# Low halves of weights made by accumulating transfers, a reload on another queue, and 32-row operands padded to 128 rows

## The chip, the core and the metric

The kernel runs on one core of a Trainium2 chip. The core has a matrix engine (TensorE, PE in the profile), a vector engine (VectorE, DVE), a scalar engine (ScalarE, ACT), a general engine (GpSimd, POOL) and SyncE (SP), which here only issues transfers. Each engine works through its own queue of instructions in order; semaphores order them among each other. Sixteen DMA engines carry the transfers; SP's go through hardware queues, POOL's through a queue that its software fills. The metric is the device time of one execution in microseconds, the median of the runs.

## The reference

One layer, in float32, for a prompt of 512 tokens and 32 sample tokens (8 sequences of 4), 544 columns in all:

```python
x = x + 0.5 * swiglu(rms_norm(x), ffn1_gate, ffn1_up, ffn1_down)
h = rms_norm(x)
z = h @ w_in            # q, k, v of 8 attention heads; q, f, i and gate of 4 recurrent heads
x = x + concat(moba(q_a, k_a, v_a), gate * norm(hgrn2(q_b, f_b, i_b))) @ w_out
x = x + 0.5 * swiglu(rms_norm(x), ffn2_gate, ffn2_up, ffn2_down)

def swiglu(x, w_gate, w_up, w_down):
    return (silu(x @ w_gate) * (x @ w_up)) @ w_down
```

The model width is 1024, the hidden width of the feed-forward nets 2816. `moba` is attention; the sample tokens attend to 1024 past keys and values that lie in a paged cache (pages of 128, found through a page table), and to the sequence's own new ones. `hgrn2` is a gated linear recurrence with a state of 128 x 128 per head. New keys, values and states are outputs too.

## The kernel before

Activations stand transposed: 128 features on the partitions, 544 columns, in two halves of 272. Every large product in float32 is made of three products in a faster format: a number is split into a high part (rounded to that format) and a low part (the rest), and high x high, low x high and high x low are summed in PSUM (`products`, line 608). So PE runs chains of 272-column matrix products `xh,whi`, `xl,whi`, `xh,wlo`.

A weight block of 128 x 512 numbers (256 KB) is a unit. SP loads it into a tile `raw` (`w_load`, line 516), ACT casts it into `whi`, and DVE subtracts, `wlo = raw - whi`:

```python
def split_unit(self, src, nk, x):                       # line 530
    hi, lo = self.take_slot(x, (F32R, F32R))
    nc.scalar.copy(hi[:, :nk], src[:, :nk])
    nc.vector.tensor_tensor(lo[:, :nk], src[:, :nk], hi[:, :nk].bitcast(F32), op=ALU.subtract)
```

`w_pump` (line 572) keeps up to four split units (`AHEAD`) ready before PE asks for them. In the feed-forward nets the gate and up products of the first five hidden blocks are plain (two units each); from block 5 on (`NREG`) gate and up are done together as seven products in place of eight ("paired": `paired_gemm`, line 645), which needs sums of four weight quarters, `S` (two on DVE, two on POOL, in `w_split`, line 537), and sums of activation tiles (`right_factors`, line 661, whose steps `PACE` spreads over time).

The mixing layer (400 to 787 us) multiplies by `w_in` (28 jobs of two units), runs the attention and the recurrence as their columns arrive, and multiplies by `w_out` (8 jobs of two units). For the sample tokens POOL gathers 32 tiles of K and 32 of V, 128 x 1024 each, from the paged cache (`KV<-cache_k,idx`, `KV<-cache_v,idx`). Small products there: `kn`,`qh` and `kn`,`ql` are the prompt's scores, per pair of heads; `KV,PT` the sample's weighted values from the cache, `vs,PO` those of its own new values (32 rows); `s,hqp` the recurrence's output from the state, `hVs,ats` from its own new values (32 rows); `fc,y_qk` spreads the root factors of 32 tokens over the columns. At the layer's end the residual that was spilled after FFN 1 is reloaded, `y<-xs` (line 1769), by POOL's queue.

The order of all instructions is set before the kernel is built, by a planner inside the kernel's own program (`Order`, `Engine`, `Pool`): it simulates the engines with modelled costs, and writes each engine's instructions out in the order of modelled start times. A transfer costs its engine 0.06 us in this model. The profile attributes all instructions to one line, 284, where they are issued; so they are told apart by their tiles.

## Time and profile before

| | us |
|---|---|
| median of 3 runs (lowest to highest) | 1205.38 (1205.19 to 1206.52) |
| the profiled execution | 1210.65 |
| its span on the core | 1208.9 |
| PE busy | 1178.1 (97%) |
| DVE busy | 858.5 (71%) |
| ACT busy | 551.9 (46%) |
| POOL busy | 228.3 (19%) |
| DMA: SP's queue / POOL's queue, share of the 16 engines | 30.6% / 9.1% |

The span is what lies between the first and the last instruction of the core; the execution's time is 1.75 us longer. A matrix product of 272 columns is listed with 0.29 us, but products overlap: the next starts 0.125 us later. Stages: reading of x and start 0 to 20 us, FFN 1 to 400, the mixing layer 400 to 787, FFN 2 from 787 on.

### The profile page before, as it was taken

The numbers are of one execution on the slowest core, as the hardware profiler recorded it, in microseconds if no ns is written. First come the engines' busy times: TensorE is split into PE (matmuls) and PEld (weight loads), VectorE is DVE, ScalarE is ACT, GpSimd is POOL, SyncE is SP. The second block draws the span as 40 slices with busy tenths as digits, with TensorE's granted clock in tenths as the row PEclk, the third lists the DMA queues.
The fourth block names the chain that finished last, engine by engine and source line by source line (L and its number), as shares of the span: only waits on it lengthen the run. The fifth ranks groups of instructions, "written<-read, shape, count | busy, mean of one in ns | idle before, by whom it ended". The sixth has DMA issues, their size and how long they took to land.

```text
span 1208.9 us, 26320 instructions
## 1 busy us (share of the span) xinstructions
PE 1178.1 (97%) x10571; PEld 1113.7 (92%) x10571; DVE 858.5 (71%) x1729; ACT 551.9 (46%) x1125; POOL 228.3 (19%) x211
## 2 busy tenths in 40 slices
PE   8999999999999999989999999899999999999998
PEld 8989999999999988878878867799999999999998
DVE  6988559954875698877776557667977488736843
ACT  6455246532654345554556433344554266524632
POOL 3012012200202401000332344220020023102200
PEclk9999999999999999989999999899999999999999
DMA  5244453333314642322565776352344323323222
GB/s 161 79 123 114 133 148 97 97 106 87 87 54 135 193 129 69 97 72 74 181 195 160 235 262 222 111 158 79 93 118 131 97 81 104 106 87 88 63 79 82
DMA packets 216238, 144.74 MB, mean 120 GB/s; under 512 B 12035, under 2 KB 204067, under 8 KB 216116
## 3 DMA queue, kind: packets, MB, share of 16 engines
q1 hardware_dynamic: 205588, 106.60, 30.6%
q0 software_dynamic: 10432, 36.32, 9.1%
q8 instruction: 83, 1.36, 0.5%
q14 instruction: 39, 0.32, 0.1%
q10 hardware_dynamic: 96, 0.14, 0.0%
HBM read 133.94 MB, written 11.83 MB: 121 GB/s over the span
## 4 chain that ended last, share of the span: by engine, by line
PE 77%; DVE 13%; ACT 3%; DMA 3%; issue 2%; SPq 1%; POOL 0%; DVEq 0%; ACTq 0%; POOLq 0%
PE mm L284 51%; PE sm L284 26%; DVE wlo L284 3%; DVE xl L284 2%; DVE xwl L284 1%; DMA raw<-ffn_down 1%; ACT xh L284 1%; DVE t_h L284 1%; SPq L284 1%; ACT whi L284 1%; DVE hl L284 1%; ACT sq L284 1%; DMA raw<-ffn_up 1%; DVE S L284 1%; DMA KV<-cache_v,idx 1%
## 5 line engine op out<-in xcount | busy, mean ns | idle before, releaser
L284 PE MATMUL mm<-xh,whi 128*128 128x272 f32 x1216 | 365.0, 300 | 1.0 <-DVE t_g L284 0.5
L284 PE MATMUL mm<-xl,whi 128*128 128x272 f32 x1216 | 352.4, 290 | 5.4 <-DVE xl L284 5.2
L284 PE MATMUL mm<-xh,wlo 128*128 128x272 f32 x1216 | 353.2, 290 | 1.1 <-DVE wlo L284 1.1
L284 ACT CAST whi<-raw 128x512 fp32r<-128x512 f32 (+1 forms) x230 | 138.7, 604 | 261.4 <-PE mm L284 192.3
L284 PEld LDWEIGHTS mm<-xh,whi 128*128 128x128 f32 x1216 | 231.5, 190 | 18.2 <-issue 15.7
L284 PEld LDWEIGHTS mm<-xl,whi 128*128 128x128 f32 x1216 | 231.3, 190 | 6.4 <-DVE xl L284 6.2
L284 PEld LDWEIGHTS mm<-xh,wlo 128*128 128x128 f32 x1216 | 231.0, 190 | 2.1 <-DVE wlo L284 2.1
L284 DVE TENSOR_TENSOR wlo<-raw,whi 128x512 fp32r<-128x512 f32 (+1 forms) x230 | 165.1, 727 | 81.0 <-ACT whi L284 77.4
L284 POOL TENSOR_TENSOR S<-raw,raw 128x512 f32<-128x512 f32 x18 | 30.4, 1691 | 380.9 <-DMA raw<-ffn_up 261.1
L284 PE MATMUL mm<-hh,whi 128*128 128x272 f32 x352 | 101.5, 288 | 0.3 <-DVE x L284 0.3
L284 PE MATMUL mm<-hh,wlo 128*128 128x272 f32 x352 | 101.1, 287 | 0.0
L284 PE MATMUL mm<-hl,whi 128*128 128x272 f32 x352 | 101.1, 287 | 0.0
L284 PE MATMUL mm<-xwh,xh 128*128 128x272 f32 x296 | 85.4, 288 | 1.3 <-DVE t_h L284 0.8
L284 PE MATMUL sm<-xwl,xh 128*128 128x272 f32 x296 | 85.3, 288 | 0.0
L284 PE MATMUL mm<-xwl,xh 128*128 128x272 f32 x296 | 85.3, 288 | 0.0
L284 PE MATMUL sm<-xwh,xh 128*128 128x272 f32 x296 | 85.2, 288 | 0.0
L284 PE MATMUL mm<-xwh,xl 128*128 128x272 f32 x296 | 85.2, 288 | 0.0
L284 PE MATMUL sm<-xwh,xl 128*128 128x272 f32 x296 | 85.2, 288 | 0.0
L284 DVE TENSOR_TENSOR xl<-S,xh 128x512 fp32r<-128x512 f32 x84 | 66.0, 796 | 4.1 <-ACT xh L284 3.7
L284 PEld LDWEIGHTS mm<-hh,whi 128*128 128x128 f32 x352 | 66.3, 188 | 0.7 <-ACT whi L284 0.5
L284 ACT CAST xh<-S 128x512 fp32r<-128x512 f32 x84 | 51.8, 620 | 32.7 <-DVE S L284 13.7
L284 PEld LDWEIGHTS mm<-hh,wlo 128*128 128x128 f32 x352 | 66.2, 188 | 0.0
(325 smaller groups left out, 2639.2 us busy)
## 6 DMA issues: line engine op xcount, KB each, us to landing
raw<-ffn_down SPq DMA_DIRECT2D x64, 256.0 KB
raw<-ffn_gate SPq DMA_DIRECT2D x56, 256.0 KB
raw<-ffn_up SPq DMA_DIRECT2D x56, 256.0 KB
raw<-w_in SPq DMA_DIRECT2D x56, 256.0 KB
raw<-ffn_down SPq DMA_DIRECT2D x32, 192.0 KB
xl<-ffn_gate SPq DMA_DIRECT2D x16, 256.0 KB
xh<-ffn_up SPq DMA_DIRECT2D x16, 256.0 KB
xl<-ffn_up SPq DMA_DIRECT2D x16, 256.0 KB
```

Of the source, the lines that this page charges most:

```text
L284: call(*map(real, args), **{k: real(v) for k, v in kw.items()})
```

## The change

1. *Low parts.* For the 72 units of `w_in` and `w_out`, and for the second unit of the plain gate and up jobs of both feed-forward nets (18 units), the low part is no longer subtracted by DVE. ACT writes `-raw`, rounded to the fast format, into `wlo`, and POOL issues a transfer that adds `raw` to it. In the mixing layer up to six units are made ahead (`AHEAD_MIX`).
2. *Paired jobs.* They now hold five `raw` tiles. Two of the four sums are DVE additions in place, one is a POOL sum, and one is an accumulating transfer; signs are turned accordingly in `hidden_paired`. `right_factors` makes its tiles in other pieces (a class `Factors`; 14 DVE operations, of which more are half as wide, in place of 10, and `PACE` 1.1 in place of 0.8).
3. *The reload* `y<-xs` goes to SP's queue.
4. *Padding.* `vs`, `hVs`, `ats` and `PO` get 128 partitions, of which the upper 96 are filled with zeros once; the products with them, and the one with `y_qk`, run with 128 rows.
5. Of the first hidden block, `up` is read from PSUM directly (two DVE copies less); the planner's model has other costs for transfers issued by POOL; the base of weight slots grows from 4 to 6, and the memory for POOL's descriptors is set to 8192 bytes.

```diff
 HT = T // 2
-PACE = 0.8
+AHEAD_MIX = 6
+PACE = 1.1
...
-                s = self.order.dma(self.part, 4 * args[1].shape[0] * self.free(args[1]), names)
+                pool = self.part == "pool"
+                s = self.order.dma(self.part, 4 * args[1].shape[0] * self.free(args[1]), names,
+                                   1.3 if pool else 0.06, 3.0 if "accum_op" in kw else 1.5)
...
-        self.nc.sync.dma_start(raw[:, :job["nk"]], job["src"][len(job["raw"])])
+        raw_k = raw[:, :job["nk"]]
+        i = len(job["raw"])
+        if job["paired"]:
+            parts = [r[:, :job["nk"]] for r, _ in job["raw"]]
+        if job["src"][i] is None:
+            self.nc.gpsimd.tensor_tensor(raw_k, parts[0], parts[1], op=ALU.add)
+        else:
+            self.nc.sync.dma_start(raw_k, job["src"][i])
+            if job["paired"] and i == 2:
+                self.nc.gpsimd.dma_start(raw_k, parts[0], accum_op=ALU.add)
+        if job["paired"] and i == 3:
+            self.nc.gpsimd.dma_start(parts[1], raw_k, accum_op=ALU.add)
...
-    def split_unit(self, src, nk, x):
+    def split_unit(self, src, nk, x, transfer=False):
+
         nc = self.nc
         hi, lo = self.take_slot(x, (F32R, F32R))
         nc.scalar.copy(hi[:, :nk], src[:, :nk])
+        if transfer:
+            nc.scalar.activation(lo[:, :nk], src[:, :nk], AF.Identity, scale=-1.0)
+            nc.gpsimd.dma_start(lo[:, :nk], src[:, :nk], accum_op=ALU.add)
+            return hi, lo, x
         nc.vector.tensor_tensor(lo[:, :nk], src[:, :nk], hi[:, :nk].bitcast(F32), op=ALU.subtract)
...
-            self.units.append(self.split_unit(job["raw"][n][0], nk, x))
+            self.units.append(self.split_unit(job["raw"][n][0], nk, xs[0], job["mixer"] or n == 1 and job["start"]))
...
-            nc.tensor.matmul(p3[64 * h:64 * h + 64, :NS], r[96:128, 18 + h:19 + h].to_broadcast([NS, 64]),
-                             self.ident[96:128, 96:128], start=True, stop=True)
+            nc.tensor.matmul(p3[:, NS * h:NS * h + NS], r[:, 18 + h:19 + h].to_broadcast([128, 128]),
+                             self.ident[:, 96:128], start=True, stop=True)
...
-        self.vs = mp.tile([NS, 512], F32, name="vs")
+
+        self.vs = mp.tile([128, 512], F32, name="vs")
+        self.Vs = mp.tile([128, 128], F32, name="hVs")
+        self.ats = mp.tile([128, 2 * NS], F32, name="ats")
+        self.PO = mp.tile([128, 128], F32, name="PO")
+        for x in (self.vs, self.Vs, self.ats, self.PO):
+            nc.gpsimd.memset(x, 0.0)
...
-                nc.gpsimd.dma_start(x[k], xspill[k])
+                nc.sync.dma_start(x[k], xspill[k])
...
-    nc = bacc.Bacc("TRN2", target_bir_lowering=False, num_devices=1)
+    nc = bacc.Bacc("TRN2", target_bir_lowering=False, num_devices=1, dynamic_dma_scratch_size=8192)
```

How this moves instructions is shown at three places. Numbers behind a tile's name only tell copies apart.

DVE at the third pair of attention heads, before (`z` are columns of the projection, `kn` the normed keys that PE waits for, `ql` low parts of the queries):

```order
L284 TENSOR_TENSOR z_6991<-mm_6822,R_5311 128x272
L284 TENSOR_TENSOR z_6991<-mm_6925,R_5311 128x272
L284 TENSOR_TENSOR wlo_7005<-raw_6742,whi_6954 128x512
L284 TENSOR_TENSOR wlo_7016<-raw_6751,whi_6977 128x512
L284 SCALAR_TENSOR_TENSOR kn_1288_7010<-sm_6997,qkg,kn_1288_7010 64x512
L284 TENSOR_TENSOR ql_7027<-qn_6937,qh_1289_6994 64x512
L284 SCALAR_TENSOR_TENSOR kn_1290_7025<-sm_6997,qkg,kn_1290_7025 64x512
```

The same place after:

```order
L288 TENSOR_TENSOR z_6996<-mm_6859,R_5322 128x272
L288 TENSOR_TENSOR ql_7008<-qn_6934,qh_1245_6990 64x512
L288 TENSOR_SCALAR KS<-sm_7019,qkg 128x32
L288 SCALAR_TENSOR_TENSOR kn_1244_7023<-sm_7013,qkg,kn_1244_7023 64x512
L288 SCALAR_TENSOR_TENSOR kn_1246_7030<-sm_7013,qkg,kn_1246_7030 64x512
L288 TENSOR_TENSOR ql_7008<-qn_6934,qh_1247_7005 64x512
```

The two subtractions that stood ahead of `kn` are gone from DVE's queue there, and `KS`, the sample's keys, has come ahead of it.

ACT at the second pair of heads, before (`kt` keys, `qh` high parts of the queries):

```order
L284 COPY kt_6490<-sm_6444 128x512
L284 COPY kt_6490<-sm_6463 128x128
L284 CAST whi_6521<-raw_6210 128x512
L284 CAST whi_6548<-raw_6361 128x512
L284 CAST qh_1195_6560<-qn_6440 64x512
L284 ACTIVATE kn_1194_6575<-sm_6562,qkg 64x512
```

The same place after:

```order
L288 CAST whi_6548<-raw_6420 128x512
L288 ACTIVATE wlo_6558<-raw_6420 128x512
L288 CAST whi_6576<-raw_6439 128x512
L288 ACTIVATE wlo_6584<-raw_6439 128x512
L288 ACTIVATE kn_1158_6591<-sm_6579,qkg 64x512
```

Behind each cast of a weight tile stands now the negation into `wlo`, so four instructions on weights stand ahead of `kn` in place of two.

POOL between the gathers of V for the sample tokens, before:

```order
L284 DMA KV_9798<-cache_v,idx 128x1024
L284 DMA KV_10037<-cache_v,idx 128x1024
L284 DMA KV_10058<-cache_v,idx 128x1024
L284 DMA KV_10085<-cache_v,idx 128x1024
L284 DMA KV_10122<-cache_v,idx 128x1024
L284 TENSOR_TENSOR at_10171<-oS_9967,fc 128x512
```

And in the changed kernel, at a like place:

```order
L288 DMA KV_9840<-cache_v,idx 128x1024
L288 DMA wlo_9777<-raw_9318 128x512
L288 DMA wlo_9864<-raw_9335 128x512
L288 DMA KV_9888<-cache_v,idx 128x1024
L288 DMA wlo_9928<-raw_9480 128x512
L288 DMA wlo_10006<-raw_9509 128x512
L288 DMA KV_10081<-cache_v,idx 128x1024
```

The accumulating transfers of low parts stand in POOL's queue between the gathers, here four around one gather.

## Rows read from the trace of the kernel before

Instructions of the kernel before; times in us from the span's start unless marked ns.

**Rows 1.** The page's part 1 (busy time, share of the span, instructions of each engine) and part 4 (the chain that ended last, by engine):

```profile
PE 1178.1 (97%) x10571; PEld 1113.7 (92%) x10571; DVE 858.5 (71%) x1729; ACT 551.9 (46%) x1125; POOL 228.3 (19%) x211
...
PE 77%; DVE 13%; ACT 3%; DMA 3%; issue 2%; SPq 1%; POOL 0%; DVEq 0%; ACTq 0%; POOLq 0%
```

**Rows 2.** The table by stretch: start and end, length, then busy us (and instructions) of each engine, TensorE's granted clock, share of the DMA engines, GB/s:

```profile
20.00:60.00 40.00, 39.67 (x315) 39.10 (x315) 34.08 (x72) 20.08 (x36) 6.01 (x5) 1.00 0.25 69
60.00:120.00 60.00, 57.12 (x440) 55.25 (x439) 52.74 (x88) 33.06 (x66) 10.84 (x8) 1.00 0.45 120
160.00:400.00 240.00, 239.68 (x1910) 239.03 (x1910) 174.48 (x284) 118.25 (x229) 46.40 (x32) 1.00 0.34 98
440.00:580.00 140.00, 134.68 (x1012) 117.64 (x1011) 115.02 (x297) 72.84 (x173) 11.18 (x11) 0.95 0.29 85
580.00:690.00 110.00, 109.00 (x1414) 89.44 (x1416) 76.16 (x196) 57.84 (x137) 37.59 (x42) 1.00 0.63 195
690.00:760.00 70.00, 67.09 (x1079) 50.71 (x1079) 44.56 (x122) 21.97 (x59) 30.25 (x32) 1.00 0.72 239
760.00:787.00 27.00, 21.51 (x218) 19.46 (x217) 16.51 (x42) 10.41 (x27) 4.80 (x9) 0.87 0.31 92
...
845.00:920.00 75.00, 73.06 (x579) 72.39 (x578) 63.50 (x109) 39.00 (x75) 10.73 (x8) 1.00 0.38 109
```

**Rows 3.** The same table for two stretches inside the mixing layer whose granted clock is 0.50:

```profile
531.60:541.80 10.20, 8.78 (x29) 7.03 (x30) 7.12 (x22) 3.82 (x11) 0.00 (x0) 0.50 0.28 79
767.10:773.90 6.80, 4.37 (x19) 4.37 (x20) 5.14 (x13) 0.65 (x1) 0.00 (x0) 0.50 0.12 35
```

**Rows 4.** The timeline of PE at two places with small products (start, us, line, operation, tiles, rows and columns of the array used, shape):

```profile
466.88 0.42 PE L284 MATMUL sm<-s,hqp 128*32 128x128 f32 x8
467.24 0.42 PE L284 MATMUL sm<-hVs,ats 32*32 32x128 f32 x8
...
468.30 0.71 PE L284 MATMUL sm<-hV,at 128*128 128x128 f32 x4
...
762.58 1.52 PE L284 MATMUL sm<-KV,PT 128*32 128x128 f32 x48
```

**Rows 5.** Groups of PE's instructions by line and shape (count, busy us and mean ns of one, idle time before them and its cause):

```profile
L284 PE MATMUL sm<-vs,PO 32*32 32x128 f32 x64 | 4.2, 279 | 0.8 <-issue 0.6
...
L284 PE MATMUL sm<-hVs,ats 32*32 32x128 f32 x64 | 3.4, 280 | 0.0
...
L284 PE MATMUL sm<-fc,y_qk 32*64 32x32 f32 x16 | 1.2, 228 | 0.0
```

**Rows 6.** Groups of instructions by line and shape on DVE, ACT and POOL, columns as in the group before:

```profile
L284 DVE TENSOR_TENSOR wlo<-raw,whi 128x512 fp32r<-128x512 f32 x198 | 147.3, 755 | 63.3 <-ACT whi L284 59.9
L284 ACT CAST whi<-raw 128x512 fp32r<-128x512 f32 x198 | 122.2, 619 | 228.8 <-PE mm L284 172.0 <-issue 34.7 <-DVE y_n L284 5.0
L284 POOL DMA_INDIRECT KV<-cache_v,idx x32 | 31.5, 984 | 43.5 <-PE sm L284 40.0 <-issue 1.2 <-PE mm L284 0.8
L284 POOL TENSOR_TENSOR S<-raw,raw 128x512 f32<-128x512 f32 x18 | 30.4, 1691 | 380.9 <-DMA raw<-ffn_up 261.1 <-PE mm L284 52.6 <-DVE wlo L284 41.3
```

**Rows 7.** The table by stretch for the subtractions that write `wlo` alone (DVE's busy time and their count, granted clock, DMA share, GB/s):

```profile
440.00:580.00 140.00, 19.06 (x24) 0.95 0.29 85
580.00:690.00 110.00, 10.69 (x14) 1.00 0.63 195
690.00:760.00 70.00, 4.87 (x7) 1.00 0.72 239
```

**Rows 8.** Timelines of DVE and then of PE at the third pair of heads (in brackets the idle time before, and what ended it):

```profile
527.95 2.65 DVE L284 TENSOR_TENSOR wlo<-raw,whi 128x512 fp32r<-128x512 f32 x2
530.62 0.74 DVE L284 SCALAR_TENSOR_TENSOR kn<-sm,qkg,kn 64x512 fp32r<-64x512 f32 x1
...
529.54 0.29 PE L284 MATMUL mm<-xh,wlo 128*128 128x272 f32 x1
533.02 0.55 PE L284 MATMUL sm<-kn,qh 128*128 128x256 f32 x1 [3.19 <-DVE kn L284]
```

**Rows 9.** Timelines of DVE and of PE at the end of the mixing layer:

```profile
765.09 0.69 DVE L284 TENSOR_TENSOR wlo<-raw,whi 128x512 fp32r<-128x512 f32 x1
...
769.53 0.59 PE L284 MATMUL mm<-xl,whi 128*128 128x272 f32 x1 [3.10 <-DVE xl L284]
```

**Rows 10.** The group of POOL's instructions that reload `y`:

```profile
L284 POOL DMA_DIRECT2D y<-xs x8 | 4.4, 580 | 22.2 <-PE mm L284 22.2
```

**Rows 11.** DMA queue 0 in 690 to 760 us (the one POOL issues to: packets, MB, share of 16 engines), the gathers issued there, and the chain of waits there by line:

```profile
q0 software_dynamic: 4015, 14.62, 61.2%
...
KV<-cache_v,idx POOLq DMA_INDIRECT x29
...
by line: PE sm L284 46.0%; PE mm L284 19.2%; DMA KV<-cache_v,idx 9.3%; issue 5.4%; DVE sst L284 3.6%; ACT SC L284 2.9%; DVE hkh L284 1.6%; POOL KV L284 1.3%; DVE hqh L284 1.1%; DVE hs L284 1.1%; DVE hf L284 1.1%; DVE sq L284 1.0%; DVE rec L
```

**Rows 12.** The timeline of POOL among the gathers of V:

```profile
707.54 0.94 POOL L284 DMA_INDIRECT KV<-cache_v,idx  x1 [0.72 <-PE sm L284]
709.12 0.94 POOL L284 DMA_INDIRECT KV<-cache_v,idx  x1 [0.65 <-PE sm L284]
```

**Rows 13.** The timeline of POOL (its last four sums of squares) and of PE (the first product of the next unit) at the start of FFN 1:

```profile
19.30 6.85 POOL L284 TENSOR_TENSOR sqsum<-sqsum,sq 128x544 f32<-128x544 f32 x4 [0.71 <-ACT sq L284]
...
27.51 0.29 PE L284 MATMUL mm<-xh,whi 128*128 128x272 f32 x1
```

More of the change, by code (lines that the diff above doesn't have):

```diff
@@ L455, in quarters, with turns, job @@
                     for r in (r0, r0 + h)]
-        def plain(m, nk, r0, c0):
-            out.append({"paired": False, "src": quarters(m, nk, r0, c0), "nk": nk // 2, "raw": [], "done": 0})
-        def ffn(p):
+        def turns(m, nk, r0, c0):
+            rows = m[128 * r0:128 * (r0 + nk), c0:c0 + 128].rearrange("(k two p) m -> two p k m", two=2, p=128)
+            return [rows[0], rows[1]]
+        def job(kind, src, nk):
+            out.append({"kind": kind, "src": src, "nk": nk // 2, "raw": [], "done": 0, "paired": kind is not None, "mixer": False})
@@ L461, in ffn, with plain, paired @@
+        def plain(m, nk, r0, c0, mixer=False, start=False):
+            job(None, quarters(m, nk, r0, c0), nk)
+            out[-1]["mixer"] = mixer
+            out[-1]["start"] = start
+        def paired(kind, nk, a11, a12, a21, a22, transfer):
+            job(kind, [a11, a21, a21 if transfer else None, a22, a12], nk)
+            out[-1]["transfer"] = transfer
+        def ffn(p, pairs):
             gate, up, down = (a[p + n][0] for n in ("_gate", "_up", "_down"))
-            for g0, ng in FGROUPS:
+            for g0, ng in FGROUPS[pairs]:
@@ L463, in ffn @@
                 for f in range(g0, g0 + ng):
                     if f < NREG:
-                        plain(gate, KD, 0, 128 * f)
-                        plain(up, KD, 0, 128 * f)
-                    else:
-                        out.append({"paired": True, "nk": KD // 2, "raw": [], "done": 0,
-                                    "src": quarters(gate, KD, 0, 128 * f) + quarters(up, KD, 0, 128 * f)})
-                for m in range(KD):
-                    plain(down, ng, g0, 128 * m)
-        ffn("ffn1")
+                        plain(gate, KD, 0, 128 * f, start=True)
@@ new lines, in ffn @@
+                        plain(up, KD, 0, 128 * f, start=True)
+                    else:
+                        paired("a", KD, *quarters(gate, KD, 0, 128 * f), *quarters(up, KD, 0, 128 * f), pairs)
+                for m in range(0, KD, 2):
+                    if pairs:
+                        paired("a", ng, *turns(down, ng, g0, 128 * m), *turns(down, ng, g0, 128 * (m + 1)), True)
+                    else:
+                        plain(down, ng, g0, 128 * m)
+                        plain(down, ng, g0, 128 * (m + 1))
@@ L474, in weight_jobs @@
+        ffn("ffn1", False)
         for n, j in IN_ORDER:
-            plain(a["w_in"][0], KD, 0, COLS[n] + 128 * j)
+            plain(a["w_in"][0], KD, 0, COLS[n] + 128 * j, True)
         for m in range(KD):
-            plain(a["w_out"][0], KD, 0, 128 * m)
-        ffn("ffn2")
+            plain(a["w_out"][0], KD, 0, 128 * m, True)
+        ffn("ffn2", False)
         return out
     def room(self, kind, job):
-        free = [x for x in self.slots[kind] if x["used"] < x["bufs"] and (x["extra"] is None or job["paired"])]
+        free = [x for x in self.slots[kind] if x["used"] < x["bufs"] and x["extra"] in (None, job["kind"])]
@@ L572, in w_pump, with ahead @@
     def w_pump(self):
-        while (len(self.units) < AHEAD and self.w_split()) or self.w_load():
+        def ahead():
+            mixer = self.splitting < len(self.jobs) and self.jobs[self.splitting]["mixer"]
+            return len(self.units) < (AHEAD_MIX if mixer else AHEAD)
+        while (ahead() and self.w_split()) or self.w_load():
             pass
@@ L654, in paired_gemm @@
             for k in range(nk):
-                xh, xl = xw[k]
-                self.products(ps[b], w, k, xh[:, r], xl[:, r], first and k == 0, k == nk - 1, not first)
+                f = xw[k]
+                self.products(ps[b], w, k, f.hi(r), f.lo(r), first and k == 0, k == nk - 1, not first)
                 yield
@@ L852, in ffn, with add @@
                 yield from self.gemm(xg, KD, up)
+            if pairs:
+                for m in range(0, KD, 2):
+                    yield from self.paired_gemm(hs, ng // 2, self.down_paired(pool, x, m, done if last else lambda m: None))
+                continue
             yield from self.settle()
-            if g0 + ng == NFF:
+            if last:
                 self.fewer_slots()
             for m in range(KD):
-                def add(p, h, m=m):
+                def add(p, h, m=m, last=last):
                     c = self.cols(h)
                     nc.vector.scalar_tensor_tensor(x[m][:, c], p, 0.5, x[m][:, c], op0=ALU.mult, op1=ALU.add)
-                    if h and g0 + ng == NFF:
+                    if h and last:
                         done(m)
                 yield from self.gemm(hs, ng, add, both=m == 0)
+        if pairs:
+            self.fewer_slots()
     def setup(self):
```

260 lines of the change are left out of this document (161 added, 99 removed).

## The prediction, made before the changed kernel ran

> **What bounds the kernel now.** I read the shares of the engines and of the chain first. [rows 1] TensorE (PE) is busy 1178.1 of 1208.9 us and 77% of the chain that ended last is PE; VectorE (DVE) follows with 13%. So an edit pays only where PE waits, or where PE's own instructions become cheaper. The table by stretch then shows where PE waits [rows 2]: in the steady part of the first feed-forward net (160 to 400 us) not at all, 239.68 of 240 us, and there, as in its like in the second, nothing that the change moves can show. PE is idle for 0.33 us in 20:60, 2.88 us in 60:120, 1.94 us in 845:920, and, in the mixing layer, 5.3 us in 440:580, 1.0 us in 580:690, 2.9 us in 690:760, 5.5 us in 760:787. That is some 20 us, plus what the clock costs: two stretches of 10.2 and 6.8 us show a granted clock of 0.50, the lower of its two levels, 1.2 against 2.4 GHz [rows 3]. Both begin inside the longest waits of PE in the layer [rows 8, 9]. The sum below is made against the profiled execution, 1210.65 us (span 1208.9 and 1.75 around it); the median of the three timed runs, 1205.38, is 5.3 lower, and I subtract the same change from it.
>
> **The change, part by part.**
>
> *Padded operands.* The products with `vs`,`PO` and `hVs`,`ats` (32 partitions) and the broadcast of `y_qk` get 128 rows. Their number stays. What changes is seen in the starts on PE [rows 4]: groups of eight `s,hqp` (128 rows) and eight `hVs,ats` (32 rows) alternate, four groups from 466.88 to 468.30, thus 0.355 us per group with one change of row count each. Forty-eight `KV,PT`, all of 128 rows, take 1.52 us, of which about 0.27 is the length of the last, so 1.25 / 47 = 0.027 us each, and eight would take 0.21. A change of row count therefore costs about 0.355 - 0.21 = 0.14 us. There are 64 records of `vs,PO` in groups of eight, 64 of `hVs,ats` in groups of eight, and 16 of `y_qk` in groups of four [rows 5]: 20 groups, 40 changes, 40 x 0.14 = 5.6 us at most. I take 0.11 each, -4.4 us, since a group with other operands may pay something of it anyway. Ends: -5.6 to 0 (a loss is excluded: the number of products stays, and 128 rows run at 0.027 us a start). The Trainium skill speaks against this term: "TensorE: Matmul & The Clock Gate", section "Why this matters for your kernels", has a single matmul of 32 rows take the same time as one of 128. By that rule alone the term is nothing and the sum 4.4 us smaller; the durations in the rows agree with it, the starts between groups do not, and I go by the starts.
>
> *Low parts in the mixing layer.* 72 units lose a DVE subtraction and gain an ACT negation and an accumulating transfer on POOL's queue. A subtraction takes 0.76 us and ACT's cast 0.62 [rows 6]; there are 24 in 440:580, 14 in 580:690, 7 in 690:760 [rows 7]. DVE is off PE's path for most of them, so 72 x 0.76 = 55 us of DVE do not come back as time. Three places do.
> First, the third pair of heads [rows 8]: DVE runs two subtractions from 527.95 that last 2.65 us, and only then `kn`, at 530.62; PE, done with its projection at 529.54, waits 3.19 us for `kn`. In the new order nothing of the weights stands ahead of this `kn`, on DVE or on ACT. 2.65 us are gone; what is late next is `kn`'s own ACT step and 0.74 us on DVE, about the time PE arrives. I take -2.7 (0 to -3.2).
> Second, the clock. The 10.2 us at 0.50 begin at 531.6, inside that wait [rows 3, 8], and hold 8.78 us of PE work, of which half, 4.4 us, is the low level. Whether the level still falls when PE pauses there for some tenths of a microsecond only, these rows don't tell. I take half, -2.2 (0 to -4.4).
> Third, the end of the layer [rows 9]: a subtraction of 0.69 us at 765.09 stands in DVE's row ahead of the last head's root and `xl`, for which PE waits 3.10 us until 769.53. Its place can go: -0.7 (0 to -0.7; ACT's `xh` may be late next, since ACT now has a negation there).
>
> *What this adds.* ACT gets 72 x 0.62 = 45 us in 387; at 52% in 440:580 it has room [rows 2], but ahead of the second pair's `kn` it now runs cast, negation, cast, negation. POOL gets 72 issues of 0.58 (the plain reload) to 0.98 us (a gather) [rows 6, 10], in one queue with the gathers: a low part waits behind a gather that waits for PE to free its tile, and a gather behind a low part that waits for ACT. The transfers themselves are not in the trace. In 690:760, 29 gathers and little else took 61.2% of 70 us of all engines by POOL's DMA queue [rows 11], 1.5 us each for 512 KB (128 x 1024 numbers), so a low part of 256 KB takes 0.75 us, or 1.5 if its second reading counts like a transfer. In 580:690, 14 of them ask 10 to 21 us, and 0.37 x 110 = 41 are free: hidden, and PE has work (0.99 busy). In 690:760, 7 ask 5 to 10 us where 0.28 x 70 = 20 are free, but the gathers of V run without a gap there, 1.6 us apart [rows 12], and 9.3% of the chain, 6.5 us, is their transfers. Here I take +2 (0 to +10).
>
> *The starts of the feed-forward nets.* 18 low parts leave DVE, 13 us of work that is nearly all beside PE: PE's idle time there is 0.33 + 2.88 + 1.94 us [rows 2]. Against it stand about 1.6 us more in `right_factors` (an estimate: 14 DVE operations in place of 10 on each of four tiles, most of them half as wide, 0.4 us a tile) and, in each paired job, one POOL sum of 1.69 us replaced by a transfer [rows 6]. I take -1 (-3 to +2). In FFN 1 the first low part is issued behind POOL's last sum of squares, which ends at 26.15 us [rows 13], and the plain product after it begins at 27.51: an issue and a transfer of 0.6 + 0.75 us and their way are late by +1 (0 to +2).
>
> *No cost.* The reload of `y` moves from POOL (4.4 us in all, after 22 us of waiting for the layer's pools) to SP [rows 10]; the products of `w_out`, whose inputs are ready, stand on PE while it runs. The zero fills run once on POOL while it is idle. If the reload is late, PE's first sum of FFN 2 shows it: 1 to 2 us, taken into the range.
>
> The sum: -4.4 - 2.7 - 2.2 - 0.7 + 2 - 1 + 1 = -8.0, so 1202.6 for a profiled execution and **1197.4** for the median.
>
> **The rivals.**
> *A, the V gathers become the bound (slower).* For it speaks that they already follow each other without a gap and that POOL's order now has low parts in pairs between them; against it, that 46 of 70 us of the chain there are PE's. Each of 7 low parts would push the gathers by its issue and its transfer, 0.98 + 1.5 = 2.5 us: +17 instead of +2. It decides once the transfers' share in 690:760, now 0.72, comes near 1. Sum: -8 + 15 = +7, 1212.4.
> *B, nothing comes of it.* The wait for `kn` only changes its owner, ACT's negations in place of DVE's subtractions, the clock falls as before, and the padding gives nothing: -8.0 + 2.7 + 2.2 + 4.4 = +1.3, 1206.7. ACT's new order at the second pair of heads speaks for it, the third pair's against it.
> *C, only the padding's term is nothing.* -8.0 + 4.4 = -3.6, 1201.8. The equal durations of 32-row and 128-row records speak for it, the starts against it. The rule of the Trainium skill named above would have it so.
> *D, the low parts do not land in time at all.* A transfer takes several times my 1.5 us; then PE waits for `wlo` throughout the layer, 72 times 0.3 us or more: +22, 1219 or worse. Against it, six units are made ahead, of 24 matrix products each, at 239.68 / 1910 = 0.125 us each [rows 2]: 18 us of slack.
>
> **How the numbers follow.** Forecast 0.42, C 0.14, B 0.15, A 0.2, D 0.09. Adding the ends on the good side, -5.6 - 3.2 - 4.4 - 0.7 - 3 = -17, gives 1188; on the other side A gives 1212. 1189 to 1214 leaves out about 2 in 10. The forecast's own range is 1190 to 1203. A measurement of this kernel tells 0.2%, 2.4 us, from no change. Faster than 1203.0 holds the forecast and most of C: 0.55. B lies within 0.2%, with a little of the other cases: 0.16. A and D are slower: 0.29.
>
> **What would show it.** In the profile after: `sm<-vs,PO` with 128 rows and starts of its groups near 0.2 us apart in place of 0.35; no wait of PE for `kn` above 1 us, and one stretch at 0.50 fewer; in 690:760 a transfer share under 0.9 and PE busy 67 us or more. A wait of PE or its weight loads for the transfer that fills `wlo`, above 5 us in all, or gathers more than 2 us apart in the V stretch, would make the forecast wrong.

## The result

The changed kernel takes 1217.58 us (median of 4 runs, 1216.11 to 1217.90), the kernel before, run beside it, 1205.89 (1205.19 to 1206.52): a ratio of 1.0095, with a 95% interval of 1.0077 to 1.0112. That is 11.7 us slower where I had forecast 8 us faster, and above the whole range I gave.

The page of the changed kernel, its parts 1 and 3 (against [rows 1]):

```profile
PE 1175.2 (97%) x10571; PEld 1118.4 (92%) x10571; DVE 779.5 (64%) x1662; ACT 601.0 (49%) x1223; POOL 283.2 (23%) x293
...
q0 software_dynamic: 27648, 66.60, 24.1%
```

DVE lost 79 us of work, ACT gained 49, POOL 55, and the queue that POOL fills went from 9.1 to 24.1% of the engines. PE has 3 us less to do and yet the span is 7 us longer: PE waits more. Where, is seen in two views. First the table by stretch (columns as in [rows 2]; the first row is the layer's beginning, the fifth its end and the reload):

```profile
400.00:440.00 40.00, 35.01 (x422) 33.69 (x421) 19.50 (x54) 14.24 (x26) 23.35 (x35) 1.00 0.98 225
440.00:580.00 140.00, 137.59 (x1117) 122.35 (x1115) 103.11 (x285) 90.77 (x207) 34.67 (x37) 0.99 0.60 145
690.00:760.00 70.00, 67.81 (x1139) 53.11 (x1131) 42.93 (x124) 31.74 (x86) 39.45 (x40) 1.00 0.95 288
60.00:120.00 60.00, 55.79 (x418) 54.89 (x416) 49.07 (x85) 30.66 (x61) 12.53 (x11) 0.94 0.63 155
760.00:800.00 40.00, 27.76 (x229) 25.99 (x230) 15.47 (x39) 13.56 (x23) 6.28 (x7) 0.87 0.52 139
860.00:930.00 70.00, 66.22 (x512) 65.30 (x511) 53.14 (x93) 35.62 (x69) 13.95 (x13) 0.98 0.61 152
```

The layer's beginning in the kernel before:

```profile
400.00:440.00 40.00, 38.02 (x489) 36.51 (x488) 29.08 (x75) 10.73 (x20) 13.84 (x21) 1.00 0.59 180
```

The middle of the mixing layer got better: 137.59 of 140 us busy in 440:580, where before it was 134.68, at a granted clock of 0.99 in place of 0.95. But PE stands idle for 12 us in 760:800 (5.5 in 760:787 before), 4.2 in 60:120 (2.9 before), 3.8 in 860:930 (1.9 in 845:920 before) and 5.0 in 400:440 (2.0 before), where the DMA engines are busy nearly all the time (0.98; 0.59 before).

Second, progress: the start of the n-th of the 7656 matrix products of 272 columns, which every kernel of this study has. I read it from the traces; differences to the kernel before in us. Around 3000 to 4300 the order of products among the layer's parts differs a little between kernels, at the other marks the same work is done.

```text
product        400   600  2900  3500  4400  4500  5200  5300  7656
before, at    70.2  98.7 390.4 504.8 786.2 798.8 890.1 902.7 1203.2
changed       -0.7  +3.8  +2.8  +4.3  -8.3  +4.0  +2.8  +8.9  +7.7
e1            -0.8  +1.7  +0.6  +5.9  -1.4  +6.3  +5.0 +13.8 +12.5
e2            -0.3  +3.6  +2.5  +5.2  +3.6  +4.1  +3.0 +11.5 +10.3
e3            +0.1  -0.2  -0.1  +3.0  -1.7  -1.7  -1.7  -1.7  -1.7
e4            +5.1  +4.3  +7.2 +11.7  +3.3 +13.8 +13.8 +13.8 +12.7
e5            -1.0  +3.6  +2.5  +8.0  +1.5  +1.5  +0.3  +8.6  +7.3
e6            -0.4  +6.2  +4.4  +7.8  +1.7 +12.9 +13.3 +20.1 +18.4
e7            -1.4  +5.0  +3.6  +8.0  -0.6 +10.3  +9.6 +16.0 +14.7
e8            +1.2  +0.5  +2.5  +7.9  -1.1  -1.1  -0.6  -0.6  -2.0
e9            -1.2  -3.0  -3.0  -0.5  -9.6  +1.6  +0.4  +2.1  +1.1
e10           -1.2  +1.5  +0.4  -1.1 -12.1 -11.4 -12.6  -5.6  -6.8
e11           +0.5  -0.9  +1.3  -1.8 -13.5 -13.5 -13.7 -12.4 -13.7
e12           -0.7  -2.6  -3.1  -6.0 -18.1 -17.7 -18.8 -17.3 -18.5
```

Stages: product 2900 is near the end of FFN 1, 4400 stands in the products with `w_out`, 4500 behind the reload of `y`, and the paired jobs begin between 500 and 600 and between 5200 and 5300. In the row of the changed kernel the mixing layer gains 11.1 us (from +2.8 to -8.3); the reload loses 12.3 in one step; the starts of the paired jobs lose 6.1 each (the first from -2.4 at product 500). The profiled execution of the kernel before was 5 us above its median, that of the changed kernel within 0.3 of it; so the traces are 7.3 us apart where the medians are 11.7. The other traces are as uneven: that of e3 was taken 3.4 us above its kernel's median, that of e9 3.1 above, that of e11 4.0 below. And each edit makes the planner order all instructions anew, so a stage that an edit does not touch can shift too: e11 loses 2.2 us in FFN 1 (from -0.9 to +1.3), where none of its low parts stand. A few microseconds of a trace's difference are therefore never decided by the traces alone; the timed ratios decide.

The chain of waits over the reload in the changed kernel (start, length, what released the next):

```profile
779.68 0.52 POOL wlo L288
780.20 5.19 DMA wlo<-raw
...
786.92 3.43 DMA y<-xs
...
790.36 0.45 DVE y L288
```

SP's timeline there, with what it issues:

```profile
778.72 7.10 SPq L288 DMA_DIRECT2D raw<-w_out  x4
786.05 3.88 SPq L288 DMA_DIRECT2D y<-xs  x8
```

PE's timeline at the same place (in brackets the idle time before, and what ended it):

```profile
790.86 0.59 PE L288 MATMUL mm<-xh,whi 128*128 128x272 f32 x1 [9.29 <-DVE y L288]
```

A low part of `w_out` is issued by POOL at 779.68 and takes 5.19 us; only then is its raw tile free; SP's last load of `w_out` waits for that tile, and the eight reloads stand behind the load in the same queue. They go out at 786.05, and PE waits 9.29 us. The kernel before issued them at 782.70, though its PE was 8 us further behind at that point (POOL's timeline):

```profile
782.70 4.39 POOL L284 DMA_DIRECT2D y<-xs  x8 [22.20 <-PE mm L284]
```

### The profile page after: what moved, and what is told of

It is laid out like the page before. It is cut to its first block, busy times and chain, and to the rows that moved or that the text cites. A ratio compares the mean times of both kernels' runs of the same rounds, so it can differ in the third digit from the quotient of the medians.

```text
span 1216.1 us, 26501 instructions
## 1 busy us (share of the span) xinstructions
PE 1175.2 (97%) x10571; PEld 1118.4 (92%) x10571; DVE 779.5 (64%) x1662; ACT 601.0 (49%) x1223; POOL 283.2 (23%) x293
## 3 DMA queue, kind: packets, MB, share of 16 engines
q0 software_dynamic: 27648, 66.60, 24.1%
## 4 chain that ended last, share of the span: by engine, by line
PE 88%; DVE 4%; issue 3%; DMA 3%; ACT 2%; POOL 1%; SPq 0%; POOLq 0%; ACTq 0%
PE mm L288 60%; PE sm L288 28%; DMA raw<-ffn_gate 1%; DMA KV<-cache_v,idx 1%; DMA xin<-x_prompt 0%; SPq L288 0%; DMA wlo<-raw 0%; DVE kn L288 0%; ACT wlo L288 0%; DMA y<-xs 0%; DVE wlo L288 0%; POOL wlo L288 0%; DVE xl L288 0%; DVE t_n L288 0%; DVE ql L288 0%
## 5 line engine op out<-in xcount | busy, mean ns | idle before, releaser
L288 PE MATMUL mm<-hw,whi 128*128 128x272 f32 x704 | 132.3, 288 | 0.0
L288 POOL DMA_DIRECT2D wlo<-raw x90 | 80.9, 925 | 209.9 <-ACT wlo L288 167.3
L288 PE MATMUL mm<-xw,whi 128*128 128x272 f32 x648 | 123.9, 289 | 0.7 <-ACT t_g L288 0.7
L288 PE MATMUL sm<-xw,whi 128*128 128x272 f32 x648 | 123.2, 288 | 0.8 <-ACT t_g L288 0.8
L288 PEld LDWEIGHTS mm<-hw,whi 128*128 128x128 f32 x704 | 110.2, 188 | 0.2 <-issue 0.2
L288 PEld LDWEIGHTS mm<-xw,whi 128*128 128x128 f32 x648 | 102.4, 190 | 0.9 <-ACT t_g L288 0.9
L288 PEld LDWEIGHTS sm<-xw,whi 128*128 128x128 f32 x648 | 101.9, 189 | 1.0 <-ACT t_g L288 1.0
L288 PE MATMUL mm<-hw,wlo 128*128 128x272 f32 x352 | 101.2, 287 | 0.0
L288 PE MATMUL mm<-xw,wlo 128*128 128x272 f32 x324 | 93.6, 289 | 0.0
L288 PE MATMUL sm<-xw,wlo 128*128 128x272 f32 x324 | 93.4, 288 | 0.0
```

What stands on the lines that cost most here:

```text
L288: call(*map(real, args), **{k: real(v) for k, v in kw.items()})
```

## The experiments

Times of different comparisons are not on one level (the kernel before took 1205.9 to 1212.1 us in them); so each is given as its ratio to the kernel before run beside it, with its interval, and as microseconds at 1209. On that scale the changed kernel has +11.5.

**e1: the reload back on POOL's queue.**

```diff
-                nc.sync.dma_start(x[k], xspill[k])
+                nc.gpsimd.dma_start(x[k], xspill[k])
```

> The changed kernel with the reload of y back on POOL's queue, all else kept. Theory S (SP's queue): in the changed kernel the reload stands on SP behind four loads of w_out, each of which waits until an accumulating transfer has read its raw tile; PE then waits 9.3 us for y. On POOL the reload waits for the layer's pools and for four low parts only: PE's wait for y falls to 0 to 4 us, and the median to 1208 to 1211. Rival W: w_out's low parts are late anyway and PE waits as long for them: 1215 or more.

Measured: 1.0088 (1.0059 to 1.0116), +10.6 us, with the kernel before at 1210.8 in this comparison; PE still waits 6.14 us for `y`. POOL's timeline shows why:

```profile
782.33 0.92 POOL L288 DMA_DIRECT2D wlo<-raw  x1 [20.04 <-ACT wlo L288]
...
786.57 1.73 POOL L288 DMA_DIRECT2D wlo<-raw  x2 [1.88 <-ACT whi L288]
787.89 4.19 POOL L288 DMA_DIRECT2D y<-xs  x7
```

The queue has changed, what stands ahead in it has not: four low parts of `w_out`, waiting for ACT. Neither theory fits: it is not SP's queue as such, and PE's wait is for `y`, not for a low part. In the trace the step from product 4400 to 4500 costs 7.7 us here and 12.3 in the changed kernel, so SP's queue may have a share of it; the ratios of the two kernels do not tell them apart.

**e2: all low parts of the mixing layer back on DVE, the reload on SP.**

```diff
-            plain(a["w_in"][0], KD, 0, COLS[n] + 128 * j, True)
+            plain(a["w_in"][0], KD, 0, COLS[n] + 128 * j)
...
-            plain(a["w_out"][0], KD, 0, 128 * m, True)
+            plain(a["w_out"][0], KD, 0, 128 * m)
```

> The changed kernel with the low parts of w_in and w_out back on DVE; the reload stays on SP. Theory S: DVE frees a raw tile about a microsecond after ACT, so the four loads of w_out go early, the reload with them, and PE's wait for y is under 3 us; the mixing layer loses its gain of about 8 to 9 us, so the median is 1212 to 1218, little changed by two opposite terms. Rival Q: it is SP's queue as such (the reload always comes behind loads): the wait stays at 7 us or more and the median is 1222 or more.

Measured: 1.0048 (1.0030 to 1.0067), +5.8 us. From product 4400 to 4500 it loses 0.5 us: on SP, but without transfers ahead of it, the reload is not late. The layer loses its gain as expected (+1.1 from 2900 to 4400 in place of -11.1), and what this kernel still loses lies at the paired jobs' starts (5.5 and 8.5 us in this trace). With e1 this says: the reload is late because of the low parts, whatever the queue.

**e3: the padding alone, on the kernel before.** The edit is part 4 of the change.

> The kernel before with only the padded operands. Starts in the changed kernel's trace say 0.13 us less per group of vs,PO, 0.19 per group of hVs,ats and 0.04 more per group of y_qk, eight, eight and four groups: -2.4 us, 1203.5. My prediction's term was -4.4, 1201.5; the rule that 32 rows take the time of 128 gives 0, 1205.9.

Measured: 0.9951 (0.9932 to 0.9969), -5.9 us, with 3.7 to 8.2 inside the interval. The changed kernel's trace shows the place, an answer to [rows 4]:

```profile
652.10 0.43 PE L288 MATMUL sm<-s,hqp 128*32 128x128 f32 x8
652.34 0.40 PE L288 MATMUL sm<-hVs,ats 128*32 128x128 f32 x8
652.56 0.40 PE L288 MATMUL sm<-s,hqp 128*32 128x128 f32 x8
652.78 0.40 PE L288 MATMUL sm<-hVs,ats 128*32 128x128 f32 x8
653.11 0.49 PE L288 MATMUL sm<-hV,at 128*128 128x128 f32 x2
```

Groups of eight now start 0.22 to 0.24 us apart (0.33 into `hV,at`) where it was 0.355. Counting each group with the steps into it and out of it, the 20 groups take some 2.5 us less; the rest of the measured 5.9 is not in these rows, and what makes it was not separated.

One candidate stands in e3's own trace: the wait for `kn` at the third pair is gone there too (no wait of PE for `kn` is above 0.5 us), though DVE still makes every low part. The middle of the layer in e3 (columns as in [rows 2]):

```profile
440.00:580.00 140.00, 137.22 (x1068) 121.57 (x1067) 115.56 (x302) 76.23 (x179) 12.60 (x11) 0.98 0.30 88
```

and PE at the third pair in e2, whose low parts of this layer are on DVE as well:

```profile
537.60 0.55 PE L288 MATMUL sm<-kn,qh 128*128 128x256 f32 x1 [3.68 <-DVE kn L288]
```

So with the subtractions on DVE this wait comes in the kernel before (3.19 us) and in e2 (3.68) and not in e3: it hangs on the order that the planner makes, and not on the subtractions alone.

**e4: all 72 low parts of the mixing layer by transfer, and the padding, on the kernel before** (feed-forward nets and reload as before, six weight slots, `AHEAD_MIX` 6, the planner's new costs, 8192 bytes for descriptors).

```diff
+        if transfer:
+            nc.scalar.activation(lo[:, :nk], src[:, :nk], AF.Identity, scale=-1.0)
+            nc.gpsimd.dma_start(lo[:, :nk], src[:, :nk], accum_op=ALU.add)
+            return hi, lo, x
...
-            plain(a["w_in"][0], KD, 0, COLS[n] + 128 * j)
+            plain(a["w_in"][0], KD, 0, COLS[n] + 128 * j, True)
...
-            plain(a["w_out"][0], KD, 0, 128 * m)
+            plain(a["w_out"][0], KD, 0, 128 * m, True)
```

> The kernel before with the low parts of w_in and w_out by transfer (six units ahead, six weight slots, the changed costs of POOL's transfers and 8192 bytes for descriptors) and the padding; feed-forward nets and the reload by POOL as before. Theory S: the gain that the changed kernel's trace has inside the mixing layer (11 us up to the last product before the reload) comes without the losses: 1195 to 1198. Rival W: w_out's low parts are late and give it back at the layer's end: 1203 to 1208.

Measured: 1.0098 (1.0072 to 1.0124), +11.9 us: this kernel is as slow as the whole change, with its reload on POOL and without the change's feed-forward nets; but part of that is its own. It loses 10.5 us between products 4400 and 4500, as the changed kernel does; 5 us at the very start, which is a fault of this experiment (the two added weight slots let splits of weights in among those of `x`); and 4.5 between 2900 and 3500. From 5200 to 5300, with the old paired jobs, it loses nothing.

**e5: of the changed kernel, `w_out` alone back on DVE.**

```diff
-            plain(a["w_out"][0], KD, 0, 128 * m, True)
+            plain(a["w_out"][0], KD, 0, 128 * m)
```

> The changed kernel with only the 16 units of w_out back on DVE; w_in's 56 low parts still by transfer, the reload of y still on SP. Theory L (end of the layer): whichever queue carries the reload, it stands behind low parts of w_out, which wait for ACT, which waits for PE to free a weight slot; with DVE's subtraction the raw tiles come free early, the reload goes out as soon as the layer's pools close, and PE's wait for y falls from 9.3 us under 2: 10 us less than the changed kernel, from 11.7 above the kernel before to about 1 above it. Rival P (place of the reload in the planner's order): the wait stays above 5 us and the time within 4 us of the changed kernel's.

Measured: 1.0014 (0.9998 to 1.0031), +1.7 us, 9.8 less than the changed kernel. The step between 4400 and 4500 is 0.0. Theory L holds: 16 low parts at the layer's end carry the whole price of the reload. In the same trace SP's reloads stand behind two loads only, and these are not held:

```profile
785.11 1.87 SPq L288 DMA_DIRECT2D raw<-w_out  x2
787.41 4.08 SPq L288 DMA_DIRECT2D y<-xs  x8
```

**e6: five raw tiles, five weight slots.**

```diff
-  "tags": ("raw",), "bufs": 4
+  "tags": ("raw",), "bufs": 5
...
-  "tags": ("whi", "wlo"), "bufs": 6
+  "tags": ("whi", "wlo"), "bufs": 5
```

> The changed kernel with five raw tiles in place of four and five weight slots in place of six. Theory T (five tiles of a paired job in four raw slots): at both starts of the paired jobs (75 to 105 and 885 to 915 us) ACT's casts wait for loads that could only be issued when a slot came free; with a fifth, PE's 3 to 7 us of waiting and the stretch at the lower clock go at both places: 6 to 12 us less than the changed kernel, if the layer does not lose by its five slots. Rival B (burst of loads): the eight loads that go out together when the activations' tiles come free delay the one that is needed; then the waits stay, and the time is within 3 us of the changed kernel's.

Measured: 1.0113 (1.0080 to 1.0145), +13.7 us: theory T falls. The time alone would not say so, since the layer loses by its five slots (it gains 2.7 us from product 2900 to 4400 in place of 11.1); but the second start still costs 6.8 us, and from product 400 to 600 the loss is 6.6. ACT's timeline at the first paired job names the transfer that is late now:

```profile
84.10 0.62 ACT L288 CAST whi<-raw 128x512 fp32r<-128x512 f32 x1 [5.37 <-DMA raw<-raw]
...
89.19 0.62 ACT L288 CAST whi<-raw 128x512 fp32r<-128x512 f32 x1 [1.78 <-DMA raw<-ffn_gate]
```

`raw<-raw`, the accumulating transfer of the job's own sum, issued at 77.75 (POOL's timeline), lands at 84.1, while eight loads of 256 KB go out from 77.24 to 84.11.

**e7: the 18 low parts of the feed-forward nets' starts back on DVE.**

```diff
-                        plain(gate, KD, 0, 128 * f, start=True)
-                        plain(up, KD, 0, 128 * f, start=True)
+                        plain(gate, KD, 0, 128 * f)
+                        plain(up, KD, 0, 128 * f)
```

> The changed kernel with the 18 low parts of the plain gate and up units back on DVE. Theory T: the stalls at the starts of the paired jobs do not hang on them, 0 to 2 us less than the changed kernel (1 us of it in the first 40 us). Rival S: a raw tile that is held longer by its transfer is what makes the paired job's loads late: 6 us less or more.

Measured: 1.0130 (1.0096 to 1.0164), +15.7 us. The stalls at the paired jobs stay (from +9.6 to +16.0 in FFN 2), so rival S falls; theory T had the mechanism of this edit but not its size: without these 18 transfers the kernel is 4 us slower than the changed one by the two ratios, not 0 to 2 us faster. Their intervals overlap, so that the transfers are a gain there is not shown.

**e8: padding, and `w_in` alone by transfer, on the kernel before.** As e4, without the line for `w_out`, and without splitting weights while `x` is read:

```diff
                 if n == 4 and m == 0:
-                    self.w_pump()
+                    while self.w_load():
+                        pass
```

> The kernel before with the padding and w_in's 56 low parts by transfer, w_out's on DVE, the reload on POOL, the paired jobs as before, and no splitting of weights during the reading of x (the six slots there cost 5 us in the run with all 72 low parts). Theory L: the padding's 5 us are kept, and of the 11 us that the layer gained in the changed kernel's trace most is kept too: 8 to 13 us less than the kernel before. Rival: the low parts' gain is the padding's alone: 4 to 6 us less.

Measured: 0.9979 (0.9961 to 0.9996), -2.5 us: a miss, 3.4 us worse than the padding alone. It gains 9 us from product 3500 to 4400, and has lost 5.3 between 2900 and 3500; of these, padding alone (e3) gains 4.7 and loses 3.1, since product 3500 lies where the kernels' orders differ. The chain of waits runs there, in this kernel and in the changed one, through POOL's low parts into its fill of `hs`; of the changed kernel:

```profile
429.31 0.60 ACT whi L288
429.92 0.54 ACT wlo L288
...
430.74 0.86 POOL wlo L288
431.60 0.57 POOL hs L288
432.19 0.46 DVE hs L288
...
436.67 0.38 PE sm L288 x19
```

ACT's cast and negation, POOL's issue of the low part, POOL's fill of `hs` behind it, DVE's work on `hs`, and PE. POOL's timeline there:

```profile
417.13 0.87 POOL L288 DMA_DIRECT2D wlo<-raw  x1 [4.44 <-ACT wlo L288]
417.72 0.89 POOL L288 DMA_DIRECT2D SC<-rsample  x1
...
424.01 2.27 POOL L288 COPY sbias<-SC 128x1024 f32<-128x1024 f32 x1 [4.51 <-DMA SC<-rsample]
...
427.77 2.65 POOL L288 DMA_DIRECT2D wlo<-raw  x3 [0.55 <-ACT hf L288]
430.74 0.86 POOL L288 DMA_DIRECT2D wlo<-raw  x1 [0.33 <-ACT wlo L288]
431.28 0.88 POOL L288 MEMSET hs<- 128x544 f32 x1
```

The fill of `hs`, 0.9 us of work, which waits for nobody but stands behind four low parts, ends at 432.2; and the setup of the bias ahead of it waited 4.51 us for its own transfer. That wait alone is nothing new. In the kernel before POOL waits as long for it, but there it begins 12 us earlier:

```profile
411.56 2.25 POOL L284 COPY sbias<-SC 128x1024 f32<-128x1024 f32 x1 [4.71 <-DMA SC<-rsample]
...
415.06 0.55 POOL L284 MEMSET hs<- 128x544 f32 x1
```

New is what stands ahead in POOL's order: the last of the four loads `SC<-rsample` goes out at 417.72, behind a low part that waited 4.44 us for ACT, and `hs` is filled 16 us later than before.

**e9: of the changed kernel, four raw tiles from the activations' tiles for the paired jobs, in place of ten.**

```diff
-                        self.more_slots("a", home, [f"{t}{i}" for i in range(5) for t in ("xh", "xl")],
-                                        [(f"xh{i}", f"xl{i}") for i in range(5, KD)])
+                        self.more_slots("a", home, [f"{t}{i}" for i in range(2) for t in ("xh", "xl")],
+                                        [(f"xh{i}", f"xl{i}") for i in range(2, KD)])
```

> The changed kernel whose paired jobs get four raw tiles from the activations' tiles when these come free, as before the change, in place of ten (the other tiles go to split weights). Theory B (burst of loads): at the starts of the paired jobs eight loads go out within 6 us in the changed kernel, four in the kernel before, and the one load that ACT waits for takes 4 to 6 us to land among them; with four fewer the waits of 3 us and the lower clock behind them go at one or both places: 4 to 8 us less than the changed kernel. Rival F (the paired jobs' own form: five tiles, a sum in place, a transfer in the chain): the waits stay and the time is within 2 us of the changed kernel's, or longer, since the jobs have fewer tiles for themselves.

Measured: 0.9991 (0.9973 to 1.0009), -1.1 us, 12.6 less than the changed kernel and more than I expected of it. Both starts are mended: 0.2 us less from product 500 to 600 (it was 6.1 more), 1.7 more from 5200 to 5300 (6.1). What ACT waited for, by its timeline in the changed kernel:

```profile
83.83 0.62 ACT L288 CAST whi<-raw 128x512 fp32r<-128x512 f32 x1 [2.16 <-DMA raw<-ffn_gate]
84.36 0.38 ACT L288 COPY t_g<-mm 128x272 f32<-128x272 f32 x1
88.79 0.62 ACT L288 CAST whi<-raw 128x512 fp32r<-128x512 f32 x1 [4.06 <-DMA raw<-ffn_gate]
89.32 0.38 ACT L288 COPY sq<-mm 128x272 f32<-128x272 f32 x1
```

and in e9 at the first of these two places:

```profile
82.74 0.62 ACT L288 CAST whi<-raw 128x512 fp32r<-128x512 f32 x1 [1.28 <-DMA raw<-ffn_gate]
```

In the changed kernel ACT's cast waits 2.16 and 4.06 us for a load, and behind the cast, in ACT's order, stands a copy of PE's result (`t_g`, `sq`), which PE needs done before it can go on:

```profile
84.79 0.52 PE L288 MATMUL mm<-xw,whi 128*128 128x272 f32 x2 [0.70 <-ACT t_g L288]
...
89.75 0.52 PE L288 MATMUL mm<-xw,xh 128*128 128x272 f32 x2 [3.00 <-ACT sq L288]
```

The load of the second wait was issued by SP at 83.96, behind eight loads into the activations' tiles; in e9 it goes out at 79.60, behind three (SP's timelines), and ACT does not wait for it. So theory B holds in this form: the needed load is late because of the loads ahead of it, and PE waits since ACT works in order. The edit changes a second thing, though: the six tiles that are no longer raw make three more slots for split weights. The timelines show the load going out earlier; that none of the 12.6 us comes from the added slots was not tested.

**e10: low parts by transfer for 22 of the 28 projections (44 units), `w_out` and the first six on DVE; else the changed kernel.**

```diff
-            plain(a["w_in"][0], KD, 0, COLS[n] + 128 * j, True)
+            plain(a["w_in"][0], KD, 0, COLS[n] + 128 * j, i >= 6)
...
-            plain(a["w_out"][0], KD, 0, 128 * m, True)
+            plain(a["w_out"][0], KD, 0, 128 * m)
```

> The changed kernel with w_out's low parts and those of the first six projections of w_in on DVE, 44 by transfer. Theory C (collision at the layer's start): from 400 to 440 us the DMA engines are 1.0 busy with low parts by transfer, bias loads and gathers, and POOL's queue has six to eight low parts between the loads and fills that the first recurrent head needs; the layer's first 100 us lose 5 us against the padded kernel. Without them the stage is as in the kernel before: 3 to 6 us less than the run with w_out alone on DVE, 2 to 4 us below the kernel before. Rival: the loss there is chance of the clock, the time is within 2 us of that run.

Measured: 0.9968 (0.9951 to 0.9984), -3.9 us, 5.6 less than e5. The layer's start by stretch in e5 (columns as in [rows 2]):

```profile
400.00:420.00 20.00, 18.60 (x151) 18.38 (x150) 7.91 (x22) 8.18 (x15) 10.65 (x18) 1.00 0.98 228
420.00:440.00 20.00, 15.52 (x223) 14.66 (x222) 8.75 (x24) 6.07 (x11) 12.69 (x16) 0.80 0.95 225
```

and in e10:

```profile
400.00:420.00 20.00, 19.89 (x160) 19.67 (x159) 12.70 (x30) 5.51 (x11) 9.04 (x18) 1.00 0.56 146
420.00:440.00 20.00, 20.00 (x346) 18.68 (x345) 16.87 (x45) 8.42 (x17) 10.46 (x10) 1.00 0.79 237
```

PE is busy 39.9 of 40 us in place of 34.1, the DMA engines 0.56 and 0.79 in place of 0.98 and 0.95. Theory C holds. The 0.80 in e5's second row is a stretch at the lower clock that the changed kernel's trace does not have there, so 5.6 us may be somewhat more than the changed kernel loses at this place.

**e11: the same 44 units and the padding on the kernel before.** As e8, with `i >= 6` as in e10.

> The kernel before with the padding and low parts by transfer for 22 of the 28 projections, from the seventh on. Theory C: the layer's start is as with padding alone, and the middle of the layer, where DVE is busiest, keeps the 4 us that the run with all of w_in shows between its 3500th product and the layer's end: 3 to 5 us less than padding alone, 8 to 11 us less than the kernel before. Rival N: DVE's relief is worth nothing outside chance; the same as padding alone, 4 to 7 us less than before.

Measured: 0.9924 (0.9899 to 0.9949), -9.2 us. That is 3.3 us below padding alone, with intervals that overlap a little. The traces say the same more loudly, 14.8 us gained from product 2900 to 4400 against 1.6 with padding alone, but more than half of that difference can be chance: e11's trace was taken 4.0 us below its kernel's median and e3's 3.4 above. A second pair of runs says more: e2 and e10 differ in these 44 low parts alone (and in the units made ahead that go with them), and stand at 1.0048 and 0.9968, 9.7 us apart, with intervals that do not meet. So DVE's relief in the middle of the layer is real in the changed kernel, and its size stays open between some 3 and 10 us.

**e12: e9 and e10 together.**

> The changed kernel with both: 44 low parts of w_in by transfer, four raw tiles for the paired jobs from the activations' tiles. If theories B, C and L each hold, their terms add: 10 us for w_out, 4 for the layer's start and 4 to 8 for the paired jobs' starts off the changed kernel's +11.7, thus 6 to 10 us less than the kernel before. If B fails it is 0 to 4 us less than before.

Measured: 0.9884 (0.9846 to 0.9921), -14.0 us, beyond the 6 to 10 expected. This is the best kernel of the study, some 25 us below the changed one. In its trace the reload's step is 0.4 us and the two starts -0.2 and +1.5, and PE is busy 39.9 of 40 us in 400:440. From its page:

```profile
q0 software_dynamic: 23616, 59.26, 20.9%
```

The queue that POOL fills still takes 20.9% of the engines: it is not the amount of transfers that made the change slow, but three places where transfers stood in the way of others: low parts ahead of the reload, low parts ahead of the layer's first fills and loads, and loads ahead of the load that a paired job needed.

## Why the prediction was wrong

The step that failed is the paragraph "No cost", the reload of `y`. It put the move at nothing, with 1 to 2 us in the range if the reload is late; PE waited 9.3 us for it. I looked at what it takes (4.4 us of issues) and at what PE does meanwhile, and not at what stands ahead of it on the queue it is moved to. The order of the changed kernel had it in plain sight: four loads of `w_out` ahead of the eight reloads, each into a raw tile that only a landed low part frees. e5 prices it at 9.8 us, and without low parts of `w_out` the step in the trace is 0.0 (e5) and 0.5 (e2). And e1 shows that the move to SP is not the main culprit; with the low parts in POOL's queue, staying there costs 7.7 us in the trace in place of 12.3, and by the ratio about as much.

"The starts of the feed-forward nets" was mis-sized: -1 + 1 = 0 forecast, 6 us lost at each start of the paired jobs, 12.6 together by e9's ratio. I had counted DVE and POOL operations per job, and not that ten tiles come free at one moment and eight loads then go out ahead of the one that is needed. The 1 us for FFN 1's first low part came (+1.0 at product 300 in the changed kernel, -1.3 in e7, which has no such transfers); but PE's wait there, 1.64 us, is for a step of the norm on DVE, not for a low part as I had it.

Rival A, the collision of low parts with gathers on POOL's queue and the engines, was the right mechanism at the wrong place. In 690:760, where I put it, the transfers' share rose to 0.95, beyond the 0.9 I had named, and PE was busy for 67.81 us (67.09 before): no loss. It bit at 400:440, where the share is 0.98 and POOL has fills and setup to do that a head waits for. There a low part that waits for ACT holds back what stands behind it in POOL's queue, as the prediction has it for gathers. I had not read that stretch, since the layer's start is not in my rows; e10 prices it at 5.6 us.

The terms inside the layer's middle came as forecast, but their cause is not shown. The wait for `kn` at the third pair is gone: the waits of PE in 400 to 790 us of the changed kernel have no `kn` at all, and the clock in 440:580 is 0.99. But e3 has lost this wait too, at 0.98, with every subtraction on DVE; the new order may have done it in both. That the low parts gain something in the middle is shown by e10 against e2, not by this wait. The padding was forecast at -4.4 and measures -5.9 (3.7 to 8.2), so a gain is shown. By the rule of the Trainium skill that I had weighed against it ("TensorE: Matmul & The Clock Gate", section "Why this matters for your kernels") it would have been 0, outside the interval. That the number was met is in part luck, since the starts that it was worked out from give only some 2.5. Of the 40 changes that I counted, at 0.11 us each, the steps out of 12 of the 16 groups of eight still cost 0.20 us, as the step to `hV,at` in the rows of e3, and the groups of `y_qk` got longer. What makes the rest stays open. My terms for the layer add up to -8.0 and the trace has -11.1, but 5 us of a trace can be chance. For one low part I had 0.75 or 1.5 us of all engines and went by both as ends: POOL's queue grew from 9.1% of 1208.9 to 24.1% of 1216.1 us, 183 us for 124 accumulating transfers (90 low parts and 34 sums of paired jobs), 1.48 each, and a little more, since the eight reloads left this queue. The dearer end is the true one.

Rival D did not come: no wait of PE for a low part is in the list of waits. They were in time, at 4.1 us from issue to landing; what was late was whatever stood behind them.

## What to carry to other kernels

When work moves to a transfer, its source stays occupied until the transfer has landed: follow who waits for that tile (the next load), and what is queued behind that waiter. Read the order around each moved instruction for what stands ahead of it, at the stage's ends above all, and count how many transfers are released at one moment when tiles come free together. A change that helps in a stage's middle and hurts at its edges is best applied to the middle alone: 44 of 72 low parts, with four raw tiles in place of ten, turned +11.5 into -14.0 us.

## What the runs showed of the hardware that was not expected

An accumulating transfer of 256 KB within the core's memory takes 1.5 to 1.6 us of all 16 engines, about as long as a gather of 512 KB ([rows 11], 1.5 us): 1.48 by the sum above, and 1.6 in 930 to 1216 us of the changed kernel, where twelve of them, alone on POOL's queue, take 6.7% of 286 us. Its issue costs POOL 0.93 us, and it lands 4.1 us after it; the row of the issues and of the landing:

```profile
L288 POOL DMA_DIRECT2D wlo<-raw x90 | 80.9, 925 | 209.9 <-ACT wlo L288 167.3
...
wlo<-raw POOLq DMA_DIRECT2D x90, 256.0 KB, 4.1
```

The lower level of PE's clock moved with the stalls: the changed kernel has it behind the reload and both starts of the paired jobs (10.2 us from 787, inside the stretch at 0.87 above; 6.8 from 90.5; 3.4 from 899), besides 3.4 from 469 in the layer, and no longer behind the third pair's `kn`. e12 shows it once inside the layer, and in the feed-forward nets at the first and the last microseconds only. So these stalls were paid twice: once as a wait, and again as products at 1.2 GHz behind it: after the reload they start 0.23 us apart (791.25, 791.48, 791.71) in place of 0.125.
